# Four of a chunk's seven float32r products with one 512-column pass for both parts of the operand, in granule order, with the parts at new distances and one low part made by a transfer

## The chip, the cores and the metric

The kernel runs on one NeuronCore of a Trainium2 chip. The metric is device time in microseconds of one launch, the median of several runs; lower is better. Beside the runs, one execution was recorded by the hardware profiler, and all rows shown are from that one.

## What is computed

One encoder layer: a SwiGLU feed-forward at half weight, a mixer (Fourier groups beside grouped-query attention), a second SwiGLU at half weight, and a last normalization. The change lies in the two feed-forwards, so only they are shown.

```
D_MODEL = 1024; SEQ = 512; D_FF = 2752

def swiglu(h, w_gate, w_up, w_down):
    return (jax.nn.silu(h @ w_gate) * (h @ w_up)) @ w_down

x = x + 0.5 * swiglu(rms_norm(x, ffn1_norm), ffn1_w_gate, ffn1_w_up, ffn1_w_down)
...
x = x + 0.5 * swiglu(rms_norm(x, ffn2_norm), ffn2_w_gate, ffn2_w_up, ffn2_w_down)
return rms_norm(x, final_norm)
```

All inputs and outputs are float32.

## The kernel before

**Numbers in two parts.** TensorE is fed in float32r, a rounded float32. To keep float32 accuracy every operand is split into a high part (rounded) and a low part (what is left), and a product of two operands is three passes into one sum: high x high, high x low, low x high. The high part is a cast on ScalarE, the low part a subtraction on VectorE (`lows`, L127-128), or, by `rest_by_dma` (L155-158), a negated copy on ScalarE to which a transfer from the POOL queue adds the source.

**Chunks and seven products.** A feed-forward goes through its 2752 inner columns in chunks of 128 (`j`). A few chunks are made plainly (`gate`); the other 35 (over both feed-forwards) by `seven`: gate and up weights of a chunk and the two halves of the input channels form a 2x2 block product, which needs seven block products instead of eight, named by their weights: a11, a12, s1, s2, s4, s3, a22. Their partners, made once by `operands`, are the parts b11, b21, t1, t2, b22, t3, t4 of one tile `rt`, each 256 token columns wide (`HALF`) by four blocks of 128 channels (`KH`). `multiply` (L413-423) runs one block product: 4 blocks x 3 passes of 256 columns, 84 passes a chunk. Each pass loads its weights first. The columns are taken straight. Passes of 512 columns elsewhere (down products, plain chunks) take theirs in granules: `turned` views the columns as 4 x 32 groups of 4, so that a pass goes over every fourth group of four first.

**Who else works on a chunk.** `prepare` brings the weights of chunk j+1 in (`raw_g`, `raw_u`, from SP's queue), makes the sums s1 to s4 on VectorE (L394), casts on ScalarE (L379, L388) and the low parts on VectorE (L128), into slots of one tile `ring`. `seven` spreads these over the steps of chunk j (`PIECES`). `step` takes each product out of its bank: copies on ScalarE (`kept`, L428, L456, L464), additions on VectorE (L441, L451, L457), the activation (L452), the product of gate and up (L465) and the split of that (L466, L128) into `at`, which the down products read. Bank `r` sums a11, s2, s3 and a22 one after the other, `q` sums s1 and s4, `p` holds a12; a copy must be out before the next product goes into the same bank.

**Stages.** Chunks come in groups of five or six; behind each group the down products of that group run (`down`, passes of 512 columns, line L184). So a feed-forward is a row of stages: seven products of a group (some 56 us), down products (some 33 us).

**Order.** TensorE and SP run in the order in which the program is written. The order on VectorE, ScalarE and POOL is set by a scheduler when the program is built, and within an engine it is fixed.

**Places.** Constants such as `FRONT`, `LOWER`, `NEAR`, `ASIDE` and the empty tiles of `room` shift tiles in memory by some elements. In `rt` each part occupied 2048 elements, the four blocks of its high part and then those of its low part.

## Time and profile before

| | |
|---|---|
| median of 3 runs | 820.92 us (820.88 to 820.94) |
| the profiled execution | 820.94 us |
| its span, first to last instruction | 818.9 us |
| TensorE clock granted | 1.000 |
| seven products, six stages | 46 to 56 us each |
| down products, behind each | some 28 to 33 us |

How to read the rows. A group shows line, engine, operation, output and inputs, shapes, count, then the busy time in us, the mean length of one in ns, and idle time before. A matmul's recorded length reaches from its first column to its last result, and passes overlap; the spacing of passes is shorter than their length. A timeline row gives start, length, engine, operation and how many equal instructions it merges; in brackets stands idle time and who ended it. A window row gives a stretch, its length, then busy us and count for PE, PEld (weight loads), DVE (VectorE), ACT (ScalarE), POOL, then the granted clock, DMA share and GB/s.

### The profile page before, as it was taken

Reading aid. Unit: us, or ns where it says so; the run is one execution under the profiler, and the core shown is the slowest. Engines: PE = TensorE matmul, PEld = TensorE weight load, DVE = VectorE, ACT = ScalarE, POOL = GpSimd, SP = SyncE. Lnnn points to the kernel's source line nnn. Section 1 sums busy time; section 2 is a strip of 40 time slices with the busy share of each in tenths; the row PEclk is TensorE's granted clock in tenths of the full one; section 3 lists DMA queues with packets and bytes.
Section 4 is the critical chain, followed back from the end, with each engine's and each line's share of the span. In section 5 each row is a group of like instructions: output and inputs, shape, how many; then the busy total and the mean of one; then the engine's idle time right before and its main releaser. Section 6 shows DMA issues by size and latency. Waiting matters only on the chain.

```text
span 818.9 us, 13611 instructions
## 1 busy us (share of the span) xinstructions
PE 812.4 (99%) x5362; PEld 746.1 (91%) x5362; DVE 637.5 (78%) x1003; ACT 483.1 (59%) x810; POOL 29.3 (4%) x31
## 2 busy tenths in 40 slices
PE   9999999999999999999999999999999999999997
PEld 7889999899989998889998888899989999899987
DVE  7898896479856847799998578999945896479574
ACT  7763674257523735699998448456632673257462
POOL 0110000000000000221000001100000000000001
PEclk9999999999999999999999999999999999999999
DMA  7664322333141223342101234542232322322222
GB/s 258 174 145 179 124 93 77 124 104 142 59 151 71 90 70 116 129 147 66 65 26 52 77 112 127 123 176 108 94 122 114 127 100 69 132 104 97 69 78 103
DMA packets 31568, 89.97 MB, mean 110 GB/s; under 512 B 3728, under 2 KB 9232, under 8 KB 31504
## 3 DMA queue, kind: packets, MB, share of 16 engines
q1 hardware_dynamic: 27776, 82.61, 29.1%
q0 software_dynamic: 3008, 5.51, 3.7%
q10 hardware_dynamic: 720, 0.98, 0.3%
q8 instruction: 42, 0.69, 0.3%
q14 instruction: 22, 0.18, 0.1%
HBM read 84.24 MB, written 2.10 MB: 105 GB/s over the span
## 4 chain that ended last, share of the span: by engine, by line
PE 95%; DVE 2%; ACT 1%; POOL 1%; issue 1%; DMA 0%; POOLq 0%; DVEq 0%; ACTq 0%
PE dn L184 25%; PE r L420 23%; PE q L420 12%; PE gu L184 8%; PE mix L184 6%; PE p L420 6%; PE gu L709 3%; PE mix L1203 2%; PE mix L1169 2%; PE mix L1007 1%; PE mix L1008 1%; PE mix L1009 1%; PE mix L1066 1%; PE mix L1143 1%; PE mix L1144 1%
## 5 line engine op out<-in xcount | busy, mean ns | idle before, releaser
L420 PE MATMUL r<-rt,ring 128*128 128x256 f32 x1686 | 209.2, 276 | 0.0
L184 PE MATMUL dn<-at,ring 128*128 128x512 f32 x900 | 202.5, 380 | 0.0
L420 PEld LDWEIGHTS r<-rt,ring 128*128 128x128 f32 x1686 | 200.3, 188 | 0.8
L184 PEld LDWEIGHTS dn<-at,ring 128*128 128x128 f32 x900 | 168.0, 188 | 28.3
L420 PE MATMUL q<-rt,ring 128*128 128x256 f32 x840 | 106.6, 276 | 0.0
L128 DVE TENSOR_TENSOR ring<-s,ring 128x1024 fp32r<-128x1024 f32 x70 | 85.5, 1221 | 23.8 <-ACT ring L379 20.8
L420 PEld LDWEIGHTS q<-rt,ring 128*128 128x128 f32 x840 | 100.4, 188 | 0.0
L544 DVE SCALAR_TENSOR_TENSOR gx<-dn,gx 128x512 f32<-128x512 f32 x61 | 41.9, 688 | 67.1 <-PE dn L184 67.1
L379 ACT CAST ring<-s 128x1024 fp32r<-128x1024 f32 x70 | 73.5, 1050 | 28.3 <-PE p L420 13.7
L170 ACT CAST ring<-raw_dn 128x768 fp32r<-128x768 f32 (+3 forms) x58 | 45.3, 784 | 72.8 <-PE dn L184 61.9
L128 DVE TENSOR_TENSOR ring<-raw_dn,ring 128x768 fp32r<-128x768 f32 (+3 forms) x58 | 51.5, 892 | 5.7 <-PE r L420 4.4
L420 PE MATMUL p<-rt,ring 128*128 128x256 f32 x420 | 53.3, 276 | 0.0
L128 DVE TENSOR_TENSOR ring<-raw_g,ring 128x1024 fp32r<-128x1024 f32 x35 | 42.7, 1220 | 11.7 <-PE p L420 10.2
L420 PEld LDWEIGHTS p<-rt,ring 128*128 128x128 f32 x420 | 50.2, 188 | 0.0
L184 PE MATMUL gu<-ring 128*128 128x512 f32 x216 | 48.9, 381 | 0.0
L379 ACT CAST ring<-raw_g 128x1024 fp32r<-128x1024 f32 x35 | 36.8, 1051 | 17.2 <-DMA raw_g<-in_wgu 11.5
L184 PEld LDWEIGHTS gu<-ring 128*128 128x128 f32 x216 | 40.4, 188 | 6.9
L428 ACT COPY p<-r 128x256 f32<-128x256 f32 x35 | 12.9, 369 | 44.9 <-PE r L420 44.6
L452 ACT ACTIVATE g<-g 128x512 f32<-128x512 f32 x35 | 22.2, 633 | 23.9 <-DVE g L451 23.6
L388 ACT CAST ring<-raw_u 128x512 fp32r<-128x512 f32 x35 | 21.8, 624 | 16.0 <-PE q L420 15.7
L184 PE MATMUL mix<-near,ring 128*128 128x512 f32 x120 | 28.8, 381 | 0.0
L465 DVE TENSOR_TENSOR u<-g,u 128x512 f32<-128x512 f32 x35 | 24.0, 687 | 6.1 <-ACT u L464 6.0
(266 smaller groups left out, 1314.3 us busy)
## 6 DMA issues: line engine op xcount, KB each, us to landing
raw_g<-in_wgu SPq DMA_DIRECT2D x35, 512.0 KB, 3.8
raw_u<-in_wgu SPq DMA_DIRECT2D x35, 512.0 KB, 4.3
raw_dn<-in_wd SPq DMA_DIRECT2D x40, 384.0 KB, 3.1
raw_gu<-in_wgu SPq DMA_DIRECT2D x12, 512.0 KB, 3.7
raw_o<-in_wo SPq DMA_DIRECT2D x8, 512.0 KB, 3.5
raw_dn<-in_wd SPq DMA_DIRECT2D x8, 448.0 KB, 3.7
raw_wq<-in_wins SPq DMA_DIRECT2D x4, 512.0 KB, 3.5
raw_f<-in_winf SPq DMA_DIRECT2D x4, 512.0 KB, 3.5
```

Source lines behind the costliest of these rows:

```text
L128: nc.vector.tensor_tensor(out=lo, in0=src, in1=asf(hi), op=ALU.subtract)
L170: nc.scalar.copy(hi[:, :n, :], raw[:, :n, :])
L184: nc.tensor.matmul(ps, a, b, start=first and b is mhi and a is whi, stop=last and a is wlo)
L379: nc.scalar.copy(hi, src)
L388: nc.scalar.copy(hi, src)
L420: nc.tensor.matmul(ps[:, t], a[:, ks], b[:, i, t], start=first and i == 0 and o == 0, stop=i == KH - 1 and o == 2, skip_group_check=not first,
L452: nc.scalar.activation(b["g"], b["g"], AF.Silu)
L465: nc.vector.tensor_tensor(out=u, in0=b["g"], in1=u, op=ALU.mult)
L544: nc.vector.scalar_tensor_tensor(out=x[d][:, t], in0=ps[:, t], scalar=0.5, in1=x[d][:, t], op0=ALU.mult, op1=ALU.add)
L709: nc.tensor.matmul(turned(pss[c]), w[:, k % 2, c], turned(m[k]), start=k == 0 and m is hh and w is hi, stop=k == KD - 1 and w is lo,)
L1169: nc.tensor.transpose(pts[n][:, c * P : (c + 1) * P], prob[t, b, c][:, kc * P : (kc + 1) * P], ident)
L1203: nc.tensor.matmul(turned(outs[t, b]), w, turned(p), start=kc == 0 and i == 0, stop=kc == 3 and i == 1)
```

## The change

`rt` gets a new layout: in each block the high and the low 256 columns lie side by side, and the seven parts begin `PART_AT` elements further than they would. For the four products in `WIDE` (a12, s4, s3, a22) the high weights meet the 512 columns of a block in one pass, so that high x high lands in the left half of a bank and high x low in the right half; low x high goes into the left half as a pass of 256. Both go in granules. What leaves such a bank is the sum of the halves: one more addition on VectorE each, and at s3 a copy of 512 instead of 256 elements on ScalarE. The other three products keep 3 x 4 straight passes of 256 columns, also the one split pass at the start of a stage. The low part of a22 is made by `rest_by_dma` from the weights in memory instead of a subtraction on VectorE.

```diff
+PART_AT = (0, 48, 96, 128, 180, 232, 284)
+WIDE = ('a12', 's4', 's3', 'a22')
...
-            rt = ap.tile([P, 7, 2, KH, HALF], F32R, name=f"rt{n_}")
+            rt = ap.tile([P, 7 * KH * S + PART_AT[-1] + PART_AT[-1] - PART_AT[-2]], F32R, name=f"rt{n_}")
...
-            part = {n: rt[:, i] for i, n in enumerate(("b11", "b22", "b21", "t1", "t2", "t3", "t4"))}
+            begins = [i * KH * S + o for i, o in enumerate(PART_AT)]
+            part = {
+                n: rt[:, o : o + KH * S].rearrange("p (k b) -> p k b", b=S)
+                for n, o in zip(("b11", "b22", "b21", "t1", "t2", "t3", "t4"), begins)
+            }
...
-                    lows(lo, src, hi)
+                    rest_by_dma(lo.rearrange("p (a b) -> p a b", b=P), hi.rearrange("p (a b) -> p a b", b=P), wgu[2 * j + 1][:, KH:])
...
-                    (whi, wlo), (mhi, mlo) = w[wn], (part[on][:, i] for i in range(2))
+                    whi, wlo = w[wn]
                     for i in range(KH):
-                        ks = slice(i * P, (i + 1) * P)
-                        for o, (a, b) in enumerate(((whi, mhi), (whi, mlo), (wlo, mhi))):
-                            for t in parts_of(next(count)):
-                                nc.tensor.matmul(
-                                    ps[:, t], a[:, ks], b[:, i, t], start=first and i == 0 and o == 0,
-                                    stop=i == KH - 1 and o == 2, skip_group_check=not first,
-                                )
+                        ks, m = slice(i * P, (i + 1) * P), part[on][:, i]
+                        start, stop = first and i == 0, i == KH - 1
+                        if wn in WIDE:
+                            nc.tensor.matmul(turned(ps), whi[:, ks], turned(m), start=start, stop=False, skip_group_check=True)
+                        else:
+                            for o in range(2):
+                                for t in parts_of(next(count)):
+                                    nc.tensor.matmul(
+                                        ps[:, t], whi[:, ks], m[:, o * HALF :][:, t], start=start and o == 0, stop=False,
+                                        skip_group_check=True,
+                                    )
+                        o, m = (turned(q[:, :HALF]) if wn in WIDE else q[:, :HALF] for q in (ps, m))
+                        nc.tensor.matmul(o, wlo[:, ks], m, start=False, stop=stop, skip_group_check=True)
...
+                def added(out, ps, other, n):
+                    nc.vector.tensor_tensor(out=out, in0=ps[:, :HALF], in1=other, op=ALU.add)
+                    if n in WIDE:
+                        nc.vector.tensor_tensor(out=out, in0=ps[:, HALF:], in1=out, op=ALU.add)
+
+                def kept(out, ps, wide=False):
+                    nc.scalar.copy(out, ps[:, HALF:] if wide else ps[:, :HALF])
+                    if wide:
+                        nc.vector.tensor_tensor(out=out, in0=ps[:, :HALF], in1=out, op=ALU.add)
...
+                            nc.scalar.copy(b["u"], b["r"])
+                            nc.vector.tensor_tensor(out=u, in0=u, in1=b["u"][:, HALF:], op=ALU.add)
+                            nc.vector.tensor_tensor(out=u, in0=u, in1=b["p5"], op=ALU.add)
```

How the instructions stand, at three places. A row has line, operation, output and inputs (with the chunk's number), shape, and how many of it follow each other.

On PE, in the second group, the products of chunk 11 from s1 to s3 and the first of chunk 12, before:

```order
L420 MATMUL q_11_1796<-rt_129,ring 128x256 x12
L420 MATMUL r_11_1744<-rt_129,ring 128x256 x12
L420 MATMUL q_11_1796<-rt_129,ring 128x256 x12
L420 MATMUL r_11_1744<-rt_129,ring 128x256 x12
L420 MATMUL r_12_1866<-rt_129,ring 128x256 x12
```

and now, from the end of s2 on, s4 whole and the start of s3:

```order
L436 MATMUL r_11_1671<-rt_129,ring 128x256 x2
L441 MATMUL r_11_1671<-rt_129,ring 128x256
L432 MATMUL q_11_1717<-rt_129,ring 128x4x32x4
L441 MATMUL q_11_1717<-rt_129,ring 128x4x16x4
L432 MATMUL q_11_1717<-rt_129,ring 128x4x32x4
L441 MATMUL q_11_1717<-rt_129,ring 128x4x16x4
L432 MATMUL q_11_1717<-rt_129,ring 128x4x32x4
L441 MATMUL q_11_1717<-rt_129,ring 128x4x16x4
L432 MATMUL q_11_1717<-rt_129,ring 128x4x32x4
L441 MATMUL q_11_1717<-rt_129,ring 128x4x16x4
L432 MATMUL r_11_1671<-rt_129,ring 128x4x32x4
L441 MATMUL r_11_1671<-rt_129,ring 128x4x16x4
```

Twelve passes of 256 became four pairs of 512 and 256; the three products that are not in `WIDE` still have twelve.

On DVE, the work of one chunk (12, with the weights of 13 and 14), before:

```order
L441 TENSOR_TENSOR g_12_1894<-p_12_1881,p_12_1879 128x256
L128 TENSOR_TENSOR ring<-raw_g_13_1860,ring 128x1024
L465 TENSOR_TENSOR u_11_1855<-g_11_1772,u_11_1855 128x512
L128 TENSOR_TENSOR ring<-s_0_13_1864,ring 128x1024
L128 TENSOR_TENSOR ring<-raw_u_13_1861,ring 128x512
L128 TENSOR_TENSOR at_128<-u_11_1855,at_128 128x512
L394 TENSOR_TENSOR s_0_14_1986<-raw_u_14_1983 128x512
L451 TENSOR_TENSOR g_12_1894<-q_12_1918,u_12_1945 128x256
L128 TENSOR_TENSOR ring<-s_0_13_1865,ring 128x1024
```

and now:

```order
L445 TENSOR_TENSOR g_12_1806<-p_12_1797,p_12_1783 128x256
L487 TENSOR_TENSOR u_11_1770<-u_11_1770,p_11_1718 128x256
L130 TENSOR_TENSOR ring<-raw_g_13_1776,ring 128x1024
L447 TENSOR_TENSOR g_12_1806<-p_12_1797,g_12_1806 128x256
L452 TENSOR_TENSOR u_11_1770<-r_11_1671,u_11_1770 128x256
L130 TENSOR_TENSOR ring<-s_0_13_1780,ring 128x1024
L496 TENSOR_TENSOR u_11_1770<-g_11_1695,u_11_1770 128x512
L406 TENSOR_TENSOR s_0_14_1891<-raw_u_14_1888 128x512
L445 TENSOR_TENSOR g_12_1806<-q_12_1828,u_12_1855 128x256
L406 TENSOR_TENSOR s_0_14_1891<-s_0_14_1891,raw_g_14_1887 128x512
L130 TENSOR_TENSOR at_128<-u_11_1770,at_128 128x512
L447 TENSOR_TENSOR g_12_1806<-q_12_1828,g_12_1806 128x256
```

The subtraction from raw_u is gone; additions L447 (twice) and L452 are new, and the low part of s (L130, from s_0_13) stands one addition further back.

On ACT, from the cast of a22 to the silu of chunk 11, before:

```order
L388 CAST ring<-raw_u_12_1739 128x512
L428 COPY p_11_1809<-q_11_1796 128x256
L466 CAST at_128<-u_10_1733 128x512
L428 COPY u_11_1823<-r_11_1744 128x256
L452 ACTIVATE g_11_1772<-g_11_1772 128x512
L379 CAST ring<-s_0_12_1743 128x1024
L456 COPY u_11_1855<-r_11_1744 128x256
```

and now:

```order
L400 CAST ring<-raw_u_12_1666 128x512
L450 COPY p_11_1718<-q_11_1717 128x256
L159 ACTIVATE ring<-ring 128x512
L450 COPY u_11_1744<-r_11_1671 128x256
L497 CAST at_128<-u_10_1659 128x512
L391 CAST ring<-s_0_12_1670 128x1024
L485 COPY u_11_1770<-r_11_1671 128x512
L479 ACTIVATE g_11_1695<-g_11_1695 128x512
```

The negated copy (L159) stands where the cast of `at` was, that cast is one copy later, and s3's copy (L485, 512 elements) stands ahead of the silu instead of behind it. On POOL 35 transfers of 128x512 are new (17 in the first feed-forward, 18 in the second), with no other instruction between them; SP's queue is the same.

44 lines of the change are left out of this document (24 added, 20 removed).

## The prediction

> **What bounds the kernel now.** First the page: busy time of each engine, the clock, and the chain of work that ended last.
>
> ```profile
> PE 812.4 (99%) x5362; PEld 746.1 (91%) x5362; DVE 637.5 (78%) x1003; ACT 483.1 (59%) x810; POOL 29.3 (4%) x31
> PEclk9999999999999999999999999999999999999999
> PE 95%; DVE 2%; ACT 1%; POOL 1%; issue 1%; DMA 0%; POOLq 0%; DVEq 0%; ACTq 0%
> PE dn L184 25%; PE r L420 23%; PE q L420 12%; PE gu L184 8%; PE mix L184 6%; PE p L420 6%; PE gu L709 3%; PE mix L1203 2%; PE mix L1169 2%; PE mix L1007 1%; PE mix L1008 1%; PE mix L1009 1%; PE mix L1066 1%; PE mix L1143 1%; PE mix L1144 1%
> ```
>
> TensorE is the chain, and L420, the line that the change rewrites, is 41% of it (23 + 12 + 6). A busy share of 99% does not yet say that passes follow without gaps, so next come the waits (PE alone) and three windows, each one chunk of the seven products long.
>
> ```profile
> PE busy L654 <- PEq L1519: 0.8, 1, 0.8
> PE mix L1143 <- DVE near L128: 0.2, 1, 0.2
> 171.20:180.72 9.52, 9.52 (x86) 9.52 (x85) 8.85 (x13) 5.45 (x11) 0.00 (x0) 1.00 0.36 117
> 180.72:190.24 9.52, 9.52 (x86) 9.52 (x85) 8.11 (x12) 6.97 (x12) 0.00 (x0) 1.00 0.29 113
> 190.24:199.76 9.52, 9.52 (x86) 9.52 (x85) 9.34 (x14) 6.53 (x12) 0.00 (x0) 1.00 0.38 134
> ```
>
> TensorE (first figure) never waits in the seven products; VectorE (third) is already busy 8.1 to 9.3 us of each 9.52, ScalarE (fourth) 5.5 to 7.0. So the change can gain only what it takes off the passes, and it can lose through passes that get longer or through VectorE.
>
> **What a pass costs.** The timeline of PE gives the spacing from long runs, and the groups by form the length of one pass.
>
> ```profile
> 224.82 26.56 PE L184 MATMUL dn<-at,ring 128*128 128x512 f32 x120
> 188.91 2.88 PE L420 MATMUL r<-rt,ring 128*128 128x256 f32 x24
> 191.63 0.62 PE L420 MATMUL p<-rt,ring 128*128 128x256 f32 x4
> L420 PE MATMUL r<-rt,ring 128*128 128x256 f32 x1674 | 209.0, 276 | 0.0
> L420 PE MATMUL q<-rt,ring 128*128 128x256 f32 x840 | 106.6, 276 | 0.0
> L420 PE MATMUL p<-rt,ring 128*128 128x256 f32 x420 | 53.3, 276 | 0.0
> L184 PE MATMUL dn<-at,ring 128*128 128x512 f32 x900 | 202.5, 380 | 0.0
> ```
>
> A 512-column pass in granule order comes every (26.56 - 0.38)/119 = 0.2200 us; a 256-column pass every (191.63 - 188.91)/24 = 0.1133 us, and 84 of them make the 9.52 us of a chunk. Two points give a line: (220.0 - 113.3)/256 = 0.417 ns a column and a fixed 6.7 ns a pass.
>
> **The change, part by part.**
> (1) *One pass for two.* In four products the high weights meet high and low part of the operand in one 512-column pass. Columns stay the same; 4 products x 4 blocks x 35 chunks = 560 passes go, each with its fixed 6.7 ns: -3.73 us. A chunk falls by 107 ns to 9.41 us. The Trainium skill (TensorE: Matmul & The Clock Gate, "Wait — 56ns, not 53.3ns?") gives a warm pass a fixed cost of about 2.5 ns beside its columns; by that the saving would be an estimated 1.4 us. The rows above do not agree with it for this kernel's float32r passes with a weight load each, and the rows decide.
>
> (2) *Pairs.* Passes now alternate, 512 then 256. The trace has such switches only where the down stage meets a last product; windows there show the first pass behind each switch.
>
> ```profile
> L420 PE MATMUL r<-rt,ring 128*128 128x256 f32 x1 | 0.3, 279 | 0.0
> L184 PE MATMUL dn<-at,ring 128*128 128x512 f32 x1 | 0.4, 384 | 0.0
> ```
>
> The 256 is 3 ns longer than its steady 276, the 512 is 4 ns longer than 380. At 7 ns for each of 560 pairs that would be +3.9 us, all of the gain. But there the order of columns changes too, from granules to straight; in the pairs both passes go in granules. The other end is the steady rows, 0. I take 0, as the order does not switch within a pair, and keep 3.9 for the range and a rival. A gain is not excluded either: the fixed 6.7 ns is far above nothing, and if new places halved it on the 1120 paired passes that would be another -3.7 us.
>
> (3) *New distances.* Counted modulo 64 elements, the parts move by 0, 48, 32, 0, 52, 40 and 28. Only b11 and t1 keep their place against the weights; t2, still in straight 256-column passes (3 x 4 x 35 = 420), and all four paired parts do not. What places do is seen in the mixer, whose tiles lie elsewhere.
>
> ```profile
> L1007 PE MATMUL mix<-ring 128*128 128x256 f32 x48 | 13.6, 284 | 0.0
> L1008 PE MATMUL mix<-ring 128*128 128x256 f32 x48 | 13.3, 277 | 0.0
> L1066 PE MATMUL mix<-pos,near 128*128 128x256 f32 x16 | 2.5, 281 | 0.0
> L184 PE MATMUL mix<-near,ring 128*128 128x512 f32 x120 | 28.8, 381 | 0.0
> L184 PE MATMUL mix<-ring 128*128 128x512 f32 x96 | 23.6, 386 | 0.0
> ```
>
> 256 columns take 277 to 284 ns there, 512 in granules 381 to 386. For t2: 0 to +5 ns (L1066), 0 to 2.1 us; I take L1008's +1 ns, the mildest row, since nothing else about t2's passes changes: +0.4 us. For the pairs 0 to +11 ns (+6 and +5), 0 to 6.2 us; I take 0.
>
> (4) *VectorE.* A 512-element subtraction for a22 goes; four 256-element additions come (a12, s4, s3, a22).
>
> ```profile
> 184.73 0.42 DVE L441 TENSOR_TENSOR g<-p,p 128x256 f32<-128x256 f32 x1
> 185.07 1.22 DVE L128 TENSOR_TENSOR ring<-raw_g,ring 128x1024 fp32r<-128x1024 f32 x1
> 187.94 0.68 DVE L128 TENSOR_TENSOR ring<-raw_u,ring 128x512 fp32r<-128x512 f32 x1
> 188.54 0.69 DVE L128 TENSOR_TENSOR at<-u,at 128x512 fp32r<-128x512 f32 x1
> 163.00:219.00 56.00, 56.00 (x495) 56.00 (x494) 49.92 (x73) 36.19 (x64) 0.00 (x0) 1.00 0.30 104
> 538.20:594.20 56.00, 56.00 (x495) 56.00 (x494) 52.69 (x79) 35.45 (x63) 0.00 (x0) 1.00 0.32 113
> ```
>
> From start to start an addition costs 185.07 - 184.73 = 0.34, the subtraction 188.54 - 187.94 = 0.60: per chunk 4 x 0.34 - 0.60 = +0.76 us, per stage of six chunks about +4.4 (the last chunk's final addition falls behind it). 49.9 becomes 54.3 of 55.4 us; in the costliest stage (538.2) 52.7 becomes 57.1, 1.7 late. What hides it is the lead: the low part of raw_g is done at 186.29, and the product that reads it starts 12 passes into the run at 188.91, at 190.27: 4.0 us. The down stages behind let VectorE catch up. So 0; without that cover it is a rival below.
>
> (5) *ScalarE and the transfer.* New per chunk: the negated copy of a22's high part and a 512- for a 256-element copy at s3.
>
> ```profile
> 186.81 0.36 ACT L428 COPY p<-q 128x256 f32<-128x256 f32 x1
> 187.06 0.62 ACT L466 CAST at<-u 128x512 fp32r<-128x512 f32 x1
> 187.75 0.37 ACT L428 COPY u<-r 128x256 f32<-128x256 f32 x1
> 187.55 1.52 PE L420 MATMUL q<-rt,ring 128*128 128x256 f32 x12
> L1174 ACT CAST ph<-mix 128x512 fp32r<-128x512 f32 x32 | 18.5, 595 | 2.8 <-PE mix L1169 2.2 <-PE mix L1203 0.3
> ring<-in_wgu POOLq DMA_DIRECT2D x3, 512.0 KB, 5.3
> ```
>
> The tightest lead is here: p5 must be out of the bank q (187.17) before the next product into it starts (187.55), 0.38 us, but what stands ahead of that copy on ScalarE is as before. The negated copy takes the place that the cast at 187.06 had, at the same 0.62, and pushes nothing that TensorE reads next: u2's copy still runs at 187.75, needed at 188.91. s3's copy gets 595 - 372 = 0.22 longer and now stands ahead of the activation; its bank is read again two products later. The transfer's 5.3 us (for twice the size) stand against more than 9.5 us until a22 is multiplied in the chunk after, and no instruction of POOL waits behind it. 0.
>
> The sum: -3.73 + 0.42 = -3.3 us. The profiled execution took 820.94 us, 818.9 of it span; that is the runs' median, 820.92, to 0.02. So 817.6.
>
> **The rivals.**
> *Places lengthen the passes (slower).* If the distance between streamed operand and loaded weights sets part of each pass, t2 and the pairs pay the mixer's rows: 2.1 + 6.2 - 3.73 = +4.6, 825.5 us. It decides from 3.73 us over 1540 moved passes, 2.4 ns each. For it: 276 against 281 and 284 at equal size; against it: 277 and 381 elsewhere. By the Trainium skill (TensorE: Matmul & The Clock Gate, "Step-by-step: what each phase is for") loading weights takes no read bandwidth from a running pass, which would leave the plain sum, 817.2; the rows of 284 and 386 ns sit badly with that.
> *The switch eats the gain.* 7 ns a pair: 820.94 - 3.73 + 3.9 + 0.4 = 821.5 with t2, 821.1 without. For it: the two rows of part 2; against it: within a pair the order of columns does not change.
> *The places are better than before.* Half of the fixed cost of the pairs gone too: 817.2 - 3.7 = 813.5. For it only that 6.7 ns is unexplained.
> *VectorE becomes the bound (slower).* The three windows give (8.85 + 8.11 + 9.34)/3 = 8.77 us a chunk, with 0.76 more 9.53 against TensorE's 9.41: once the lead of 4.0 us is spent it sets the pace, +0.12 x 35 = 4.2 above 817.2. Waits inside a chunk come on top:
>
> ```profile
> 182.05 1.23 DVE L128 TENSOR_TENSOR ring<-s,ring 128x1024 fp32r<-128x1024 f32 x1 [1.64 <-ACT ring L379]
> ```
>
> If 0.1 of such 1.64 us stays in each chunk, 3.5 more: 825. Against it: the lead is longer than what one stage adds up to, and the order of the change puts other work where this wait was.
>
> **How the numbers follow.** Forecast 0.41, better places 0.11, switch 0.12, places 0.27, VectorE 0.09. A measurement here can tell 0.2%, 1.6 us, from no change: faster 0.41 + 0.11 = 0.52, same 0.12, slower 0.27 + 0.09 = 0.36. The likeliest case by itself is 816 to 819. To leave out no more than two in ten, the range goes down to the better places, 813.5, and up past the places' 825.5 to 827.
>
> **What would show it.** Right: 4802 matmuls with their weight loads (560 fewer), a chunk in 9.41 us, paired passes at 380 and 276 ns, PE still without waits, VectorE near 98% in the stages. Wrong: paired passes or t2's (r, straight) longer than that by some ns in every chunk, or waits of PE on VectorE or ScalarE late in a stage; in either case the chunk's length in a window tells how much.

## The result and the profile after

The changed kernel takes 827.93 us (median of 4 runs, 827.23 to 829.63) against 820.93 us of the kernel before beside it (4 runs, 820.88 to 821.08): a ratio of 1.0079, 95% interval 1.0063 to 1.0094. It is slower by 7.0 us, where 3.3 us less were forecast, and lies 0.9 us above the range. The profiled execution took 829.63 us, 827.8 of it span.

The page first: busy time of PE, and the chain of work that ended last.

```profile
PE 820.3 (99%) x4802; PEld 729.8 (88%) x4802; DVE 664.5 (80%) x1108; ACT 507.1 (61%) x845; POOL 59.5 (7%) x66
PE 96%; ACT 1%; DMA 1%; DVE 1%; issue 0%; POOL 0%; POOLq 0%; DVEq 0%; ACTq 0%
```

The 560 passes are gone (4802 instead of 5362), and yet PE is busy 7.9 us longer. It is still the chain. The waits of PE say whether passes became longer or wait (waited-for engine, total, times, longest):

```profile
PE busy L685 <- PEq L1550: 0.8, 1, 0.8
PE gu L740 <- ACT ring L726: 0.5, 1, 0.5
PE dn L186 <- DVE ring L130: 0.5, 1, 0.5
```

None of them is in the seven products. Among the weight loads (PEld) two do wait there, for s3's copy on ScalarE, 0.6 us in all:

```profile
PEld r L432 <- ACT u L485: 0.6, 2, 0.4
```

That is little against 7.9 us. So the passes themselves are longer. The groups by form show all of them (L432 the 512-column passes, L436 the straight ones, L441 those with the low weights):

```profile
L432 PE MATMUL r<-rt,ring 128*128 128x512 f32 x280 | 98.9, 388 | 0.1
L432 PE MATMUL q<-rt,ring 128*128 128x512 f32 x140 | 49.5, 388 | 0.0
L432 PE MATMUL p<-rt,ring 128*128 128x512 f32 x140 | 49.1, 385 | 0.0
L436 PE MATMUL r<-rt,ring 128*128 128x256 f32 x554 | 101.9, 281 | 0.0
L441 PE MATMUL r<-rt,ring 128*128 128x256 f32 x560 | 155.9, 278 | 0.0
L436 PE MATMUL q<-rt,ring 128*128 128x256 f32 x280 | 50.1, 277 | 0.0
L441 PE MATMUL q<-rt,ring 128*128 128x256 f32 x280 | 77.5, 277 | 0.0
L441 PE MATMUL p<-rt,ring 128*128 128x256 f32 x140 | 38.5, 275 | 0.0
```

Against 380 and 276 ns, the lengths of before, these are 8 x 420 + 5 x 140 = 4.1 us for the 512s and 5 x 554 + 2 x 560 + 280 + 280 - 140 = 4.3 us for the 256s: 8.4 us, more than twice the 3.73 us that the missing passes bring. Where they are is read from the timeline of PE, here one chunk of the second group; a row is the first pass of a product (s4, s3, a11, a12, a22, s1, s2, and s4 again):

```profile
181.14 0.39 PE L432 MATMUL q<-rt,ring 128*128 128x512 f32 x1
...
182.50 0.38 PE L432 MATMUL r<-rt,ring 128*128 128x512 f32 x1
...
183.87 0.40 PE L436 MATMUL r<-rt,ring 128*128 128x256 f32 x2
...
185.28 0.39 PE L432 MATMUL p<-rt,ring 128*128 128x512 f32 x1
...
186.63 0.38 PE L432 MATMUL r<-rt,ring 128*128 128x512 f32 x1
...
187.99 0.40 PE L436 MATMUL q<-rt,ring 128*128 128x256 f32 x2
...
189.37 0.40 PE L436 MATMUL r<-rt,ring 128*128 128x256 f32 x2
...
190.80 0.39 PE L432 MATMUL q<-rt,ring 128*128 128x512 f32 x1
```

The chunk takes 190.80 - 181.14 = 9.66 us, 9.52 before and 9.41 by the forecast. The start-to-start differences give each product: s4 1.36, s3 1.37, a11 1.41, a12 1.35, a22 1.36, s1 1.38, s2 1.43 us. Before, each of the seven took 1.36 (12 x 113.3 ns); four of them should have come down to 1.333. Not one did, and a11 and s2 (t2's product), in unchanged 256-column passes, are the longest.

The rest is at the ends of the stages. Of VectorE's work there the down products show what is late; the rows are the first 18 down passes behind the second stage and the pass that follows them, before and then after.

```profile
218.83 4.12 PE L184 MATMUL dn<-at,ring 128*128 128x512 f32 x18
222.79 0.39 PE L420 MATMUL r<-rt,ring 128*128 128x256 f32 x2
```

```profile
222.53 4.44 PE L186 MATMUL dn<-at,ring 128*128 128x512 f32 x18
226.81 0.39 PE L432 MATMUL r<-rt,ring 128*128 128x512 f32 x1
```

The same 18 passes take 226.81 - 222.53 = 4.28 us instead of 3.96. The waits of the weight loads name the engine, before and then after:

```profile
PEld dn L184 <- DVE at L128: 0.4, 1, 0.4
```

```profile
PEld dn L186 <- DVE at L130: 2.1, 5, 0.4
...
PEld dn L186 <- DVE ring L130: 0.9, 1, 0.9
```

And the window of the second stage (length, then busy us and count of PE, PEld, DVE, ACT, POOL):

```profile
165.82:222.53 56.71, 56.71 (x402) 53.21 (x401) 51.99 (x87) 38.74 (x67) 5.16 (x6) 1.00 0.47 126
```

VectorE is busy 51.99 of 56.71 us, 92%, and in the window from 210 to 220 us 10.00 of 10.00: towards the end of the stage it has no slack, and what is late there comes late to the down products.

Cutting both spans at the same passes, the 8.9 us between them (827.8 - 818.9) are: the six stretches of seven products +5.35, the down products around them +2.06 (four gaps of 0.30, and 0.81 in the second feed-forward's first down products, which also wait on L130), the mixer -0.19, and +1.61 ahead of the first down product. The last is put down to that one execution: that stretch is written as before, its +1.6 is there in one of the experiments (x1) and in the others it is -0.5 to +0.1, and the median of the runs is 1.7 us below the profiled one. What is left, 7.2 us, agrees with the 7.0 us of the medians.

### The profile page after: what moved, and what is told of

Its sections match the earlier page's. It is cut to its first block, busy times and chain, and to the rows that moved or that the text cites. A ratio compares the mean times of both kernels' runs of the same rounds, so it can differ in the third digit from the quotient of the medians.

```text
span 827.8 us, 12743 instructions
## 1 busy us (share of the span) xinstructions
PE 820.3 (99%) x4802; PEld 729.8 (88%) x4802; DVE 664.5 (80%) x1108; ACT 507.1 (61%) x845; POOL 59.5 (7%) x66
## 4 chain that ended last, share of the span: by engine, by line
PE 96%; ACT 1%; DMA 1%; DVE 1%; issue 0%; POOL 0%; POOLq 0%; DVEq 0%; ACTq 0%
PE dn L186 25%; PE mix L186 8%; PE r L436 8%; PE r L441 8%; PE gu L186 8%; PE r L432 8%; PE q L436 4%; PE q L441 4%; PE q L432 4%; PE p L432 4%; PE gu L740 3%; PE p L441 2%; PE mix L1234 2%; PE mix L1200 2%; PE mix L1038 1%; PE mix L1039 1%
## 5 line engine op out<-in xcount | busy, mean ns | idle before, releaser
L441 PE MATMUL r<-rt,ring 128*128 128x256 f32 x560 | 155.9, 278 | 0.0
L441 PEld LDWEIGHTS r<-rt,ring 128*128 128x128 f32 x560 | 105.3, 188 | 0.2
L436 PE MATMUL r<-rt,ring 128*128 128x256 f32 (+1 forms) x566 | 103.0, 280 | 0.0
L432 PE MATMUL r<-rt,ring 128*128 128x512 f32 x280 | 98.9, 388 | 0.1
L130 DVE TENSOR_TENSOR ring<-s,ring 128x1024 fp32r<-128x1024 f32 x70 | 85.2, 1217 | 11.0 <-ACT ring L391 8.8
L436 PEld LDWEIGHTS r<-rt,ring 128*128 128x128 f32 x566 | 86.8, 189 | 1.6
L441 PE MATMUL q<-rt,ring 128*128 128x256 f32 x280 | 77.5, 277 | 0.0
L160 POOL DMA_DIRECT2D ring<-in_wgu x38 | 32.8, 864 | 481.5 <-ACT u L450 438.5
L432 PEld LDWEIGHTS r<-rt,ring 128*128 128x128 f32 x280 | 52.5, 188 | 10.8 <-ACT u L485 0.6
L130 DVE TENSOR_TENSOR ring<-raw_dn,ring 128x768 fp32r<-128x768 f32 (+3 forms) x58 | 51.5, 891 | 6.4 <-PE r L432 3.6
L130 DVE TENSOR_TENSOR ring<-raw_g,ring 128x1024 fp32r<-128x1024 f32 x35 | 42.7, 1220 | 14.2 <-PE p L432 12.6
L441 PEld LDWEIGHTS q<-rt,ring 128*128 128x128 f32 x280 | 52.6, 188 | 0.0
L436 PE MATMUL q<-rt,ring 128*128 128x256 f32 x280 | 50.1, 277 | 0.0
L432 PE MATMUL q<-rt,ring 128*128 128x512 f32 x140 | 49.5, 388 | 0.0
L432 PE MATMUL p<-rt,ring 128*128 128x512 f32 x140 | 49.1, 385 | 0.0
```

Of the source, the lines that this page charges most:

```text
L130: nc.vector.tensor_tensor(out=lo, in0=src, in1=asf(hi), op=ALU.subtract)
L160: nc.gpsimd.dma_start(out=lo, in_=src, accum_op=ALU.add)
L432: nc.tensor.matmul(turned(ps), whi[:, ks], turned(m), start=start, stop=False, skip_group_check=True)
L436: nc.tensor.matmul(ps[:, t], whi[:, ks], m[:, o * HALF :][:, t], start=start and o == 0, stop=False, skip_group_check=True,)
L441: nc.tensor.matmul(o, wlo[:, ks], m, start=False, stop=stop, skip_group_check=True)
```

## The experiments

Two theories on the passes were set against each other. *Place*: how far the streamed part lies from the weights, or where it lies at all, sets the length of a pass, so that what counts is where a part was moved. *Entry* (or order): what runs ahead of a pass counts, the 512 behind a 256 and the other way round, so that what counts is the order of passes. The expectations name a third, *traffic*: the new transfers and the busier engines slow TensorE's reads. Then there was the question of what VectorE, ScalarE and the transfer do by their waits.

All times stand in this table. "Beside" is the kernel before on the same chip in the same batch. Chunk and products are medians over all chunks of the profiled execution, from first pass to first pass. "Stages" is the sum of the six stretches of seven products less that of before, "down" the same for the down products around them; both in us, from one execution each. A single time says little to 2 us: the 22 runs of the kernel before beside x15 lie between 820.38 and 823.49, and x1's 826.95 holds 1.7 us of the stretch ahead of the first down product. So the columns behind the times decide.

| kernel | us (runs) | beside | chunk us | a11, a12, a22, s1, s2, s4, s3 in ns | stages | down |
|---|---|---|---|---|---|---|
| before | 820.93 (4) | | 9.520 | all 1360 | 0 | 0 |
| the change | 827.93 (4) | 820.93 | 9.666 | 1413, 1354, 1359, 1381, 1428, 1364, 1367 | +5.35 | +2.06 |
| x1_places_old | 826.95 (1) | 821.41 | 9.600 | 1367, 1348, 1347, 1411, 1413, 1356, 1358 | +2.86 | +1.80 |
| x2_places_208 | 827.83 (1) | 821.41 | 9.586 | 1364, 1383, 1366, 1364, 1360, 1383, 1366 | +3.77 | +3.40 |
| x3_no_pairs | 836.28 (1) | 821.41 | 9.880 | 1381, 1413, 1421, 1379, 1428, 1421, 1437 | +14.48 | +0.86 |
| x4_grouped | 823.51 (1) | 821.41 | 9.521 | 1377, 1337, 1366, 1377, 1360, 1338, 1366 | +0.45 | +2.37 |
| x5_straight_192 | 829.83 (1) | 821.41 | 9.733 | 1413, 1368, 1379, 1413, 1413, 1368, 1379 | +6.95 | +1.22 |
| x6_straight_208 | 826.39 (1) | 821.41 | 9.614 | 1382, 1369, 1376, 1382, 1360, 1369, 1376 | +3.48 | +2.14 |
| x7_transfer_only | 827.33 (1) | 821.41 | 9.520 | all 1360 | +5.36 | +0.95 |
| x8_before_no_cut | 820.29 (1) | 821.41 | 9.520 | all 1360 | -0.78 | +0.12 |
| x9_mirrored | 824.56 (6) | 821.38 | 9.453 | 1363, 1337, 1346, 1363, 1360, 1338, 1346 | -1.96 | +5.20 |
| x10_mirrored_224 | 831.51 (1) | 821.38 | 9.680 | 1410, 1345, 1378, 1410, 1414, 1345, 1378 | +6.30 | +3.88 |
| x11_grouped_places_of_change | 824.74 (1) | 821.38 | 9.607 | 1372, 1358, 1340, 1369, 1428, 1367, 1373 | +3.42 | +0.46 |
| x12_change_relieved | 826.93 (4) | 821.07 | 9.666 | 1413, 1354, 1359, 1381, 1428, 1364, 1367 | +6.10 | +0.56 |
| x13_mirrored_relieved | 827.13 (5) | 821.07 | 9.454 | 1363, 1338, 1346, 1363, 1360, 1338, 1346 | +0.47 | +2.83 |
| x14_relieved_no_cut | 827.74 (5) | 821.07 | 9.454 | 1363, 1337, 1346, 1364, 1360, 1338, 1346 | +0.54 | +6.07 |
| x15_one_pair_of_two | 819.75 (11) | 821.13 | 9.487 | 1360, 1338, 1346, 1363, 1360, 1360, 1360 | -1.09 | +0.06 |
| x16_before_no_cut_timed | 820.27 (12) | 821.13 | 9.520 | all 1360 | -0.78 | -0.02 |

### The places alone

The change without the pairs, all products in straight 256-column passes at the change's places:

```diff
-WIDE = ('a12', 's4', 's3', 'a22')
+WIDE = ()
```

> The changed kernel without pairs (all seven products by three straight passes of 256 columns), with the change's places and the transfer kept. Places theory: a11 and s1, whose places against the weights are those of before, at 1.36 us, the five others above it, s2 at 1.43; some 825 us or more. Switch theory: nothing switches, so all seven at 1.36 and 821 us. Traffic theory: all seven above 1.36 alike.

```profile
L436 PE MATMUL r<-rt,ring 128*128 128x256 f32 x1114 | 203.5, 281 | 0.8 <-ACT u L450 0.3 <-ACT u L489 0.2
L441 PE MATMUL r<-rt,ring 128*128 128x256 f32 x560 | 157.4, 281 | 0.0
```

The passes are those of before in size, number and order; the parts of `rt` lie elsewhere, and a22's low part still comes by the transfer, which alone leaves a product at 1360 (x7, below). Their mean length is 281 ns instead of 276, with none of the pairs' added work on VectorE. The five products whose part was moved take 1413 to 1437 ns; a11 and s1, whose parts stay at a multiple of 64 elements, 1381 and 1379, with slow first passes and then 113 ns again. s2 has in this kernel the 1428 of the change. So moving the parts, without any pair, makes the straight passes of the moved ones 4 to 6 ns longer, and t2's product takes what it takes in the change.

The other way round, the pairs at the old places:

```diff
-PART_AT = (0, 48, 96, 128, 180, 232, 284)
+PART_AT = (0, 0, 0, 0, 0, 0, 0)
```

> The changed kernel with every part back at a multiple of 64 elements (the place of before), pairs and all else as in the change. Places theory (a pass is as long as the distance between streamed and loaded operand makes it): the straight product s2 falls from 1.43 us to the 1.36 of before, and the paired products change from their 1.35 to 1.37. Switch theory (512 and 256 in turn cost 7 ns a pair wherever they lie): the paired products stay within 10 ns of 1.36. Traffic theory (the 35 transfers and the busier VectorE and ScalarE slow the reads of TensorE): s2 stays at 1.43 and all else as in the change, 827 to 828 us.

The old places give the pairs 6 to 12 ns each (1348, 1347, 1356, 1358), but none gets to 1333, and s1 and s2, whose parts are now, modulo 64 elements, where they were before, take 1411 and 1413. The place is not the whole of it.

Then the straight parts at multiples of 64 elements and the paired ones 4 elements further:

```diff
-PART_AT = (0, 48, 96, 128, 180, 232, 284)
+PART_AT = (0, 4, 4, 64, 64, 68, 68)
...
-                    for src, i0, i1 in (b[:, 1:], 0, 3), (t, 3, 7):
+                    for src, i0, i1 in (b[:, 1:2], 0, 1), (b[:, 2:], 1, 3), (t[:, :2], 3, 5), (t[:, 2:], 5, 7):
...
-                        if i0 or i < (1 if n_ else 2):
+                        if i0 > 2 or i < (1 if n_ else 2):
```

> The changed kernel with the three straight parts at a multiple of 64 elements and the four paired parts 4 elements beyond one, the place that the 512-column granule passes of the down products have against their weights; the operand copies are split for it. Places theory: 512-column passes at 220 ns as there, pairs near 333, a paired product 1.33 us, s2 1.36; a11 too if places are all, so a chunk of 9.41 us and 817 to 818 us. Switch theory: pairs at 340, paired products 1.36, a chunk of 9.52, 821 us. Traffic theory: as the change, 827 to 828 us.

All three straight products are back at 1360 to 1364, a11 and s2 gain 49 and 68 ns; the pairs are no better than in the change, a12 and s4 worse (1383). The chunk falls by 80 ns.

### The order of the passes

The same places, but in each paired product the four 512s first and then the four 256s, so that two switches are left of eight:

```diff
+                    if wn in WIDE:
+                        for i in range(KH):
+                            nc.tensor.matmul(
+                                turned(ps), whi[:, i * P : (i + 1) * P], turned(part[on][:, i]), start=first and i == 0,
+                                stop=False, skip_group_check=True,
+                            )
+                        for i in range(KH):
+                            nc.tensor.matmul(
+                                turned(ps[:, :HALF]), wlo[:, i * P : (i + 1) * P], turned(part[on][:, i, :HALF]), start=False,
+                                stop=i == KH - 1, skip_group_check=True,
+                            )
...
```

> As the kernel with paired parts 4 elements beyond a multiple of 64, but in each of the four products first the four 512-column passes and then the four of 256, so that the length changes once and not in every pass. Places theory: no different from that kernel. Switch theory: a paired product falls by three switches of 7 ns, 21 ns, to 1.34 us, some 3 us in all. Traffic theory: as the change.

The timeline of PE, s2, then s4 (its 512s and its 256s), s3 in the same way, and the first pass of a11:

```profile
186.98 0.39 PE L449 MATMUL r<-rt,ring 128*128 128x256 f32 x2
...
188.34 1.04 PE L430 MATMUL q<-rt,ring 128*128 128x512 f32 x4
189.22 0.61 PE L435 MATMUL q<-rt,ring 128*128 128x256 f32 x4
189.67 1.06 PE L430 MATMUL r<-rt,ring 128*128 128x512 f32 x4
190.57 0.63 PE L435 MATMUL r<-rt,ring 128*128 128x256 f32 x4
191.04 0.40 PE L449 MATMUL r<-rt,ring 128*128 128x256 f32 x2
```

In s4 four 512s take 189.22 - 188.34 = 0.88 us, 220 ns each as in the down products, and four 256s 0.45: together 1.33, the forecast at last (1338 in the table). s3, whose 512s come right behind s4's 256s, takes 0.90 and 0.47: its passes are longer from first to last. In the table a12 and s4 gain 46 ns by the grouping, a22 and s3 nothing, and the straight products behind a paired one (a11, s1) lose 13. Alternating thus costs 65 ns a chunk, 2.3 us; entry counts.

Two variants with the low-weight passes straight, at a multiple of 64 (x5) and at +4 (x6):

```diff
-                                turned(ps[:, :HALF]), wlo[:, i * P : (i + 1) * P], turned(part[on][:, i, :HALF]), start=False,
+                                ps[:, :HALF], wlo[:, i * P : (i + 1) * P], part[on][:, i, :HALF], start=False,
```

> The four 512-column granule passes of a paired product first, then its four low-weight passes of 256 taken straight instead of in granules, and every part at a multiple of 64 elements as in before. Entry theory (how a run of passes begins, and with it its spacing, depends on what came before: behind straight passes the 512s take 224, 220, 220, 220 ns as the down products do, behind granule passes of 256 they take 231, 222, 225, 221): all four paired products alike at 1.34 us and a11, s1 and s2 at 1.36, a chunk of 9.44, 818 to 819 us. Places theory alone: the 512s lie 4 elements off the place where they took 220, so 225 and more, paired products 1.36 or more, 821 us or more.

> The same with the paired parts 4 elements beyond a multiple of 64: right for the 512-column passes, and for straight passes of 256 a place not seen here. Places theory: 512s at 220, straight passes of 256 in the pairs at 117 to 119 as t2 had in the change, a paired product 1.35 to 1.36, a chunk of 9.50. Entry theory alone: as the kernel before this, 1.34 and 9.44.

Both lose. x5 gives the cleanest row on entry; s2, and the first pass behind it:

```profile
187.75 0.40 PE L449 MATMUL r<-rt,ring 128*128 128x256 f32 x2
...
189.16 1.06 PE L430 MATMUL q<-rt,ring 128*128 128x512 f32 x4
```

1.41 us, 117.7 ns a pass from the first to the last, where x4 has 188.34 - 186.98 = 1.36, 113.3 a pass, for the same product, by the same instructions, with t2 at the same place modulo 64 elements (in x4 it lies 64 elements further on). Such a run shows two steady spacings, and stays in the one in which it comes in. In the change a11 is such a run: 1413, all twelve passes at 117.7, behind s3 with its parts at +40 (232 modulo 64); with the passes grouped and nothing else changed (x11) it takes 1372.

> The changed kernel with its own places, but in each paired product the four 512s first and then the four 256s. Switch theory: the paired products fall by some 21 ns each to 1.33 to 1.35 us. Places theory: the 512s stay at 224 to 228 ns at these places, the products within 10 ns of 1.36; s2 at 1.43 by both.

There s2 stays at 1428, behind an s1 of 1369; so far it looks like the place alone. But in the first chunk of each stage s1 takes 1411 and s2 1400. And in x12 (below), which has the change's places and order of passes, TensorE waits once for 0.52 us ahead of an a22; the rows are the first passes of the s1, the s2 and the s4 behind it:

```profile
276.78 0.40 PE L436 MATMUL q<-rt,ring 128*128 128x256 f32 x2
...
278.19 0.39 PE L436 MATMUL r<-rt,ring 128*128 128x256 f32 x2
...
279.55 0.38 PE L432 MATMUL q<-rt,ring 128*128 128x512 f32 x1
```

Here s1 takes 1.41 us, the slow spacing, and s2 1.36 us, 113.3 ns a pass, with t2 where the change puts it. So s2's 68 ns hang on its place and on what ran ahead of it together. The new places, with all that follows from them in this order of passes, are worth 86 ns a chunk (x11 against x4), s2's 68 the largest part.

Next, a22 and s3 in mirrored order (256s first, 512s last), so that equal passes meet between a12 and a22 and between s4 and s3:

```diff
+                        order = [(whi, S), (wlo, HALF)]
+                        if wn in ("a22", "s3"):
+                            order = order[::-1]
+                        for k, (a, n) in enumerate(order):
+                            for i in range(KH):
+                                nc.tensor.matmul(
+                                    turned(ps[:, :n]), a[:, i * P : (i + 1) * P], turned(part[on][:, i, :n]),
...
```

> As the grouped kernel with paired parts 4 elements beyond a multiple of 64, but a22 and s3, which follow another paired product, take their four 256-column passes first and their four 512s last. So straight passes meet only 512s on both sides, and the row is 4 x 512, 8 x 256, 4 x 512. Entry theory: a11 and s1 fall from 1.38 to 1.36 us (116, 114, 113 ns behind 512s, as the last products of a stage had in before), a12 and s4 stay at 1.34, a22 and s3 at 1.35 to 1.37; a chunk of 9.46 to 9.48, 818.5 to 819.5 us. Places theory alone: the same places, so the grouped kernel's 9.52.

> The same with the parts of a22 and s3 at 8 instead of 4 elements beyond a multiple of 64. If the 512s that follow granule passes of 256 need another place than those that follow straight ones, a22 and s3 change from 1.35 or 1.36 by 10 ns or more, either way; if the place counts only against the weights, they get longer, since 4 elements gave 220 ns in the down products.

x9's chunk came out at 9.453 as the entry theory had it: a22 and s3 fall by 20 ns to 1346, a11 and s1 by 14. With a22's and s3's parts four elements further (x10) these two take 1378, and a11, s1 and s2, whose own parts were not moved, are all in the slow spacing again. Those three have the same instructions at the same places in both kernels, so what runs ahead of them makes the difference. But x9's time is 824.56, a ratio of 1.0041 (1.0022 to 1.0059) to before: -1.96 us in the stages, +5.20 in the down products. PE's waits say on whom:

```profile
PE dn L186 <- DVE ring L130: 1.6, 3, 0.7
PE dn L186 <- DVE at L130: 1.2, 4, 0.3
```

The split pass at the start of a stage is another place of entry:

```diff
-                            for t in parts_of(next(count)):
+                            for t in (slice(0, HALF),):
```

> The kernel before without the one pass that is split into 64 and 192 columns at the start of each stage. Entry theory: the spacing that a11 has in the change, 117.7 ns, is a second steady spacing of straight passes at the very same places; without the split the stages may fall into it and hold it, up to 84 x 4.3 = 0.36 us a chunk, 833 us. Places theory alone: the places are those of before, so 113.3 ns and 820 us, some 0.1 us a stage less for the split pass.

> The kernel before with the one split pass per stage whole, again, now timed. If the 0.13 us per stage of its one look hold (the split's second pass costs its fixed part), the time is 0.8 us less than that of the kernel before, a ratio of 0.999; if that was the spread of single runs, the ratio is 1.000.

Nothing falls into the slow spacing. Each stage is 0.13 us shorter, that is what a second pass costs, and with twelve runs the ratio is 0.9989 (0.9979 to 1.0000), as the sum of passes had it, though the interval touches no change.

### VectorE and the transfer

The kernel before with nothing but a22's low part by transfer:

```diff
-                    lows(lo, src, hi)
+                    rest_by_dma(lo.rearrange("p (a b) -> p a b", b=P), hi.rearrange("p (a b) -> p a b", b=P), wgu[2 * j + 1][:, KH:])
```

> The kernel before with one part of the change alone: the low part of a22 by a negated copy and a transfer. Places and entry theories: passes stay at 113.3 ns, a chunk at 9.52, 821 us, VectorE 21 us less busy. Traffic theory: passes get longer, 824 us or more.

```profile
PE r L420 <- ACT u L428: 2.1, 6, 1.0
...
PE r L420 <- ACT u L456: 0.5, 1, 0.5
```

But for the first passes behind a wait and the last eight products, the passes come as before, so the transfers by themselves do not slow them, and 5.9 us are lost all the same: PE waits for copies out of bank r (L428, L456), and in the chunk at 188 us such a copy stands behind the negated copy on ScalarE. In the change the scheduler has ordered ScalarE's work otherwise, and only the two short waits for s3's copy are in its seven products. The transfer costs no more than that there, by an order that this one edit alone does not get.

This trace also has the second spacing with every part at its place of before. It begins behind a wait, at s3 in the last chunk but one; the rows are that s3 with the a11 that follows, a12, and the first pass behind the stage:

```profile
766.77 3.09 PE L420 MATMUL r<-rt,ring 128*128 128x256 f32 x24 [0.32 <-ACT u L428]
769.70 1.58 PE L420 MATMUL p<-rt,ring 128*128 128x256 f32 x12
...
778.18 1.04 PE L184 MATMUL dn<-at,ring 128*128 128x512 f32 x4
```

The six products from 769.70 to 778.18 take 1.41 us each instead of 1.36, and nothing about them has changed but how they were entered. Behind the other waits in that kernel's products the passes come back to 113.3 ns; what decides between the two is not shown.

Then s3's two additions from VectorE to GpSimd, in the change, in the mirrored kernel, and there without the split pass:

```diff
-                            nc.vector.tensor_tensor(out=u, in0=u, in1=b["u"][:, HALF:], op=ALU.add)
-                            nc.vector.tensor_tensor(out=u, in0=u, in1=b["p5"], op=ALU.add)
+                            nc.gpsimd.tensor_tensor(out=u, in0=u, in1=b["u"][:, HALF:], op=ALU.add)
+                            nc.gpsimd.tensor_tensor(out=u, in0=u, in1=b["p5"], op=ALU.add)
```

> The change with one edit: s3's two additions of 128x256 (420 ns each on VectorE) go to GpSimd, where the nearest row of the same shape takes 725 ns. VectorE is busy 0.95 to 1.00 of the time while a chunk is multiplied in the change, so 0.84 us of 9.67 us per chunk come off it. Theory 1 (VectorE is late at the ends of the stages): the four gaps of some 0.30 us at the first down stages and the 0.81 us of the second FFN's first down stage shrink to under 0.1 and 0.3 us, TensorE's waits on L130 go, the chunk stays at 9.67 us: about 826.0 against the change's 827.9. Theory 2 (those gaps come from something else, or GpSimd's additions come too late in their turn and hold up the transfer behind them): 827.9 or more, with the gaps there or a wait on GpSimd in their place.

> The mirrored kernel (824.6 us, chunk 9.453 us) with the same edit. Theory 1: its waits on L130 (1.6 and 1.2 us), the second FFN's late start (+1.7) and the four gaps (+0.6 to +0.7 each) are VectorE's, which is busy about 9.3 us of each 9.45 us chunk there; with 0.84 us less most of these 5 us go, and the time is 820 to 821.5, about that of the kernel before. Theory 2 (the gaps come from elsewhere): 824 or more, chunk 9.45.

> The same without the one pass per stage that is split in 64 and 192 columns. Alone on the kernel before that took 0.13 us off each of six stages. Theory 1 (passes are added up): 0.8 us less than the kernel with the relief and the split pass, 819.5 to 820.7. Theory 2 (a run of passes keeps the spacing with which it begins, and the split is one of the places where it is set): chunk medians of a11, s1 or s2 go from 1360 to about 1413, and the time is 2 us or more above theory 1's.

In the change the gaps go: the same 18 down passes, again with the pass behind them.

```profile
220.77 4.14 PE L186 MATMUL dn<-at,ring 128*128 128x512 f32 x18
224.75 0.38 PE L432 MATMUL r<-rt,ring 128*128 128x512 f32 x1
```

3.98 us instead of 4.28; in all "down" falls from 2.06 to 0.56 us, as theory 1 had it. But VectorE did not get less busy: 666.3 us in 1038 instructions, where the change has 664.5 in 1108. Beside the additions on GpSimd its own sums take longer; one of them, in the change and then in x12:

```profile
L406 DVE TENSOR_TENSOR s<-raw_g,s 128x512 f32<-128x512 f32 x35 | 23.9, 683 | 0.2
```

```profile
L406 DVE TENSOR_TENSOR s<-raw_g,s 128x512 f32<-128x512 f32 x35 | 35.5, 1014 | 0.2
```

What did change is what stands ahead of the low part of `at`, which the down products wait for: in the change it starts 2.98 us behind the end of the stage (222.53), in x12 1.03 us behind it (220.77).

```profile
225.18 0.42 DVE L486 TENSOR_TENSOR u<-u 128x256 f32<-128x256 f32 x1
225.51 0.68 DVE L130 TENSOR_TENSOR at<-u,at 128x512 fp32r<-128x512 f32 x1
```

```profile
221.80 0.68 DVE L130 TENSOR_TENSOR at<-u,at 128x512 fp32r<-128x512 f32 x1
```

Only 1.0 us arrives in the time (826.93, 4 runs), since the stages gain 0.75 us by a longer wait for s3's copy:

```profile
PE r L432 <- ACT u L485: 0.8, 2, 0.5
```

In the mirrored kernel the edit brought nothing (827.13, its five runs from 824.11 to 828.99): "down" falls from 5.20 to 2.83, and the stages rise by 2.43 with waits on ScalarE's copies. The profiled execution is the one of 824.11, so the columns account for 3.3 of the 6.1 us that the median lies above the kernel before; the rest is not shown. So the gaps are VectorE's, as theory 1 had it, but by the order of its work there and not shown to be by its amount, and the time was missed: the scheduler orders VectorE, ScalarE and GpSimd anew for each program, and in these a wait appears elsewhere. That the amount is not all is seen in x4 and x11 too, which have all the additions of the change and, behind the four stages, gaps of 0.07 and 0.05 us in all; x4 is late instead at the first down products of the two feed-forwards, by 0.83 and 1.51 us. x14 missed as well: it was to gain 0.8 us and is at 827.74; its spacings stay fast, its waits are others (L130 4.0 us). What decides about those orders stays open.

### A version below both

If VectorE and ScalarE are the limit of these pairs, half of the pairs may be had without it. Only a12 and a22 with the 512-column pass, in mirrored order, everything else straight at multiples of 64, a22's low part by transfer, no split pass:

```diff
-PART_AT = (0, 48, 96, 128, 180, 232, 284)
+PART_AT = (0, 0, 4, 64, 64, 64, 68)
-WIDE = ('a12', 's4', 's3', 'a22')
+WIDE = ('a12', 'a22')
...
```

> Only a12 and a22 with the 512-column pass (a12: its four 512s first, a22: its four 256s first, their parts 4 elements off a multiple of 64, all other parts at multiples of 64), a22's low part by transfer, no split pass. VectorE gets 0.84 us of additions per chunk and loses 0.69 us, so 0.15 more than before, where all four by pairs give it 1.0 us less room. Theory 1 (what is lost beyond the passes is VectorE's lack of time): a12 1337, a22 1346, s1 1363, the other four 1360, chunk 9.486, 35 x 0.034 = 1.2 us less than before and 0.8 for the split pass; gaps of 0.3 to 1.0 us in all remain, so 819.5 to 820.5, below the kernel before. Theory 2 (the transfer in this order of work, or the new order of the steps itself, brings waits whatever VectorE has to do): waits on ScalarE at u or on L130 as in the relieved ones, 822 or more at the same chunk.

819.75 us (11 runs), ratio 0.9979 (0.9971 to 0.9988) to the kernel before. Its page, and the one wait of PE behind the first matmuls:

```profile
PE 810.6 (99%) x5076; PEld 734.5 (90%) x5076; DVE 642.6 (79%) x1049; ACT 505.2 (62%) x866; POOL 63.6 (8%) x71
```

```profile
PE gu L752 <- ACT ring L738: 0.5, 1, 0.5
```

PE is busy 1.8 us less than before, none of its waits is in the products or the down products, VectorE has 22 us less to do than in the change, and chunk (9.487) and products are those expected. Theory 1 had it at 819.5 to 820.5. Of the 1.4 us some 0.9 are the split pass (x16, in the same batch), the rest the pairs. By the sum the stages should have fallen by 2.0 us (1.2 and 0.8) and fell by 1.09: delays of 0.1 to 0.25 us in three chunks, and two products of 1.41 us behind one of them, are much of the difference.

## Why the prediction was wrong

*What bounds the kernel*: right. TensorE's passes set the end before and after, and the change could gain only there or lose through longer passes or VectorE. It lost by both.

*(1) One pass for two*: right in mechanism. The passes went, and where the passes kept their spacing (a12 in x4 and x9) a product fell from 1360 to 1337 ns, 5.7 ns for each of its four passes instead of 6.7. By the Trainium skill (TensorE: Matmul & The Clock Gate, "Wait — 56ns, not 53.3ns?") it would have been an estimated 2.5 ns each; the rows of x4 and x9 stay nearer to the two-point line.

*(2) Pairs and (3) new distances* are the steps that failed. The prediction put the switch at 0, the pairs' places at 0 and t2 at +0.4 us, and held b11 and t1, whose places are kept, to be unchanged. Measured in the change, against what each product should have taken (1333 or 1360): the four paired products +21, +26, +31 and +34 ns, 3.9 us over 35 chunks; t2's product +68 ns, 2.4 us; a11 +53 and s1 +21, 2.6 us. Together 8.9 us where 0.4 was taken. The first two lie near or inside the bounds that were given (10.1 for switch and places of the pairs, 2.1 for t2); the third had no term at all. That is the real hole: a pass was priced by its own place, and the runs show that what ran ahead of it counts as well, for products that the change does not touch (a11, s1 and s2 in x9 and x10, and the last chunk of x7). Nor is t2's share the place alone (x12). Why a run of passes has two spacings stays open.

The choice between the ends was also made badly. "As the order does not switch within a pair" set aside the trace's only rows on such a switch, 279 and 384, by an argument that no row bore out, and "the mildest row" for t2 was one of three.

*(4) VectorE*: the mechanism named, its price missed. The 4.0 us of lead did hide the added work inside a stage; but "the down stages behind let VectorE catch up" is not so at once: the first down products need `at` and the ring's low parts from VectorE, and were 0.30 us late behind four stages and 0.81 us at the second feed-forward's start, 2.06 us in all. The waits on L130 name VectorE, and x12 shows that what stands ahead of `at` there decides. It is not the added work alone: x11 has all of it and loses 0.46 us. VectorE was nearer to 92% than to the 98% forecast in the stages (51.99 us in the second, 54.3 forecast): its busy time grew by 27.0 us in all, 0.77 a chunk as priced, but only 2.1 of the 4.4 us fell inside that stage.

*(5) ScalarE and the transfer*: right for the change, at 0, but for 0.6 us of weight loads that wait for s3's copy. x7 shows how thin the ground was: with the order of before, the same edit costs 5.9 us.

*The rivals.* "Places lengthen the passes" came nearest, 825.5, by a price of 8.3 us for t2 and the pairs against 6.3 measured for these two. That it came so near is in part luck: it had nothing for a11 and s1 (2.6) and the down products (2.06). "The switch eats the gain" is a real part of it, 2.3 us by x2 and x4. "VectorE becomes the bound" named the right engine with another mechanism: no pass waits for it inside a chunk, the down products do. By the Trainium skill (TensorE: Matmul & The Clock Gate, "Step-by-step: what each phase is for") loading weights takes no read bandwidth from a running pass; what x3 shows is that moving the streamed parts alone lengthens passes under which weights are loaded. Whether the load is the other party was not tried, since no experiment took the loads away.

## What to carry to other kernels

In this kernel a pass had no price of its own: before an edit that moves the streamed operand or changes the order of passes, price each pass that follows too, and take the spacing from a run of the new order, not from the steady rows of the old one. When VectorE is nearly full in a stage (92% here, and all of the last 10 us), ask of added work not only whether the stage hides it but who reads VectorE's results first behind the stage. Before work is moved to another engine to relieve one, add up the busy time of both afterwards: in x12 70 additions left VectorE and its busy time stayed. And where four pairs leave no room, try two.

## What the runs showed that was not expected

- The same twelve 256-column passes, on a part at the same place, ran at 113.3 or at 117.7 ns each throughout, by what ran ahead of them: s2 in x9 and in x10, and, in one and the same kernel, the products of x7 before and behind a wait.
- A shift of the streamed part by some tens of elements made straight 256-column passes 118 to 120 instead of 113 ns (x3). One place does not suit both orders of columns: behind the same four 512s, at +4, the grouped 256s in granules run at 113 (a12 in x4), straight ones at 119 to 125 (x6).
- While GpSimd adds, VectorE is slower: in x12 the sum shown above takes 1014 ns on the mean instead of 683, and GpSimd's two additions of 128x256 1325 and 1036 ns, which took 417 on VectorE. The Trainium skill (SBUF — State Buffer, "Who interferes with whom") states that a VectorE instruction with two inputs in SBUF contends with a GpSimd instruction that reads there; the rows agree with it in kind. GpSimd's addition by itself is in no run here.
